# One of seven gate products replaced, for nine pairs of feature blocks, by seven products of quarters

## Chip, cores and metric

The kernel runs on one core of a Trainium2 chip. The metric is the device time of one execution in microseconds (us), the median of several runs. TensorE is called PE here, its weight loads PEld, VectorE DVE, ScalarE ACT, GpSimd POOL, and SP is the engine whose queue issues most DMAs.

## What is computed

One encoder block on 1024 tokens of width 1024, all in float32. Cut to its steps:

```python
h = rms_norm(x, norm1_g);  z = h @ w_in                     # 1024 x 2560
a, gate, q, k, v = split(z)
conv_out = silu(layer_norm(depthwise_conv31(a * sigmoid(gate)) + bias))
attn_out = neighbourhood_attention(rms_norm(q), rms_norm(k), v, rpb)
x = x + concat(conv_out, attn_out) @ w_out
h = rms_norm(x, norm2_g)
x = x + (silu(h @ w_gate) * (h @ w_up)) @ w_down             # D_FF = 2816
```

## The kernel before

Every matrix product is done in float32 precision out of rounded parts. An operand is split into a high part (an ACT cast to fp32r) and a low part (a subtraction, on DVE or POOL); `mac` (L110) then adds three matmuls to one PSUM tile, high x high (L112), high x low (L113) and low x high (L114). Each of them loads its own 128x128 weights.

The order on every engine is the order in which the Python program issues the instructions; nothing reorders it. Engines wait for each other through semaphores, and a tile from a pool waits until the last user of its slot is done. Pools that matter here: `G`, 25 slots of 128x1024; `ST`, 5 slots of 128x512; in PSUM `mm` (4 banks), `tp` (2 banks) and `cv` (one tile of two banks).

**First block (L522 to L543).** Eleven calls on `ones` (L250) run on PE while the first loads land; each is two matmuls in the trace. Then `four` adds, for the first two token tiles of the key projection, three matmuls per `mac` in the order k, token tile. Its operands come from `h_split` (L270, x times the norm's gain, which comes with the load of `par`) and from `take_parts` (L162, the split of the first weights `wk0`).

**Gate stage (L1204 to L1224).** Gate and up projections are one 2x2 block product by Winograd's form of Strassen's scheme: for each of 22 feature blocks `i` seven products `m1` to `m7` instead of eight, each of four `mac`s (12 matmuls of 512 columns) with the tokens as the moving operand. The blocks are ordered in 11 pairs. `product` (L1075) issues a product's matmuls, `evac` (L1086) combines its PSUM result: m1 is copied to `g` by ACT, and m6, m2, m5, m7, m3, m4 add to what is there. Banks: A for m1 and m2, B for m6, m5 and m3 (both `mm`), D for m7 and m4 (`tp`). From block 2 on the order is m1, m6, m2, m5, m7, m3, m4. After each product `prep` (L964) issues the splits for a product some four later: `t_sums` on DVE (four subtractions per block), casts on ACT, low parts on POOL. `keep` (L1118) stores the results and forms sums for the down projection.

**`s_weave` (L1033)** puts transposes of the normalised tokens' sums (`s_T`) between the matmuls of the first products; for S2 two single 512-column pieces and one double one in `cv`.

**Last tile (L1309).** The last token tile of the last product is done in two halves of 256 columns, each six matmuls into its half of the one bank `A3d`, then an add on DVE and a store.

Of the kernel before, what the change touches and what calls it, by code (L numbers as in the profile page):

```python
# [12 lines left out]
P = 128  # L13
# [17 lines left out]
def layout(v):  # L31
    f = {k: np.asarray(a)[0] for k, a in v.items()}
    w_in = f["w_in"]
    ag = w_in[:, :2 * DC].reshape(KB, P, 8, P).transpose(2, 1, 0, 3)
    qkv = w_in[:, 2 * DC:].reshape(4, 2, P, 3, 512).transpose(3, 0, 2, 1, 4)
    gu = np.stack([f["w_gate"], f["w_up"]]).reshape(2, KB, P, FB, P).transpose(3, 0, 2, 1, 4)
    wd = f["w_down"].reshape(FB, P, D)
    par = np.concatenate([
        f["norm1_g"].reshape(KB, P).T,
        f["dw_kernel"].reshape(CW, 4, P).transpose(2, 1, 0).reshape(P, 4 * CW),  # L40
        f["dw_bias"].reshape(4, P).T,
        f["conv_ln_g"].reshape(4, P).T,
        f["conv_ln_b"].reshape(4, P).T,
        np.concatenate([f["q_norm_g"]] * 2)[:, None],
        np.concatenate([f["k_norm_g"]] * 2)[:, None],
    ], axis=1)
    out = {
        "x": f["x"],
        "xt": f["x"].T.reshape(4, 2, P, 2, 512).transpose(3, 0, 2, 1, 4),
        "ag": ag.reshape(8, P, KB * P),  # L50
        "qkv": qkv.reshape(3, 4, P, 1024),
        "wo": f["w_out"],
        "gu": gu.reshape(FB, 2, P, KB * P),
        "wd": wd,
        "g2": f["norm2_g"][None],
        "rpb": f["rpb"],
        "par": par,
    }
    return {k: np.ascontiguousarray(a) for k, a in out.items()}
# [8 lines left out]
def build(ctx, tc, a):  # L68
# [47 lines left out]
    def lr(w):  # L116
        return w[:, :512], w[:, 512:]
# [19 lines left out]
    def issue():  # L137
        if pos[0] < len(chunks):
            src, name, _, _ = chunks[pos[0]]
            if pos[0] not in raws:  # L140
                raws[pos[0]] = R(name + "r")
            d = raws[pos[0]]
            if len(src.shape) == 3:
                d = d.rearrange("p (k m) -> p k m", k=src.shape[1])
            for q in (0, 1) if name == "wk0" else (None,):
                sl = slice(None) if q is None else slice(q * 512, q * 512 + 512)
                (nc.scalar if q == 0 else nc.sync).dma_start(d[:, sl], src[:, sl])
            pos[0] += 1

    def take(n=1, ahead=True):  # L150
# [70 lines left out]
    def load_xt(h, kp, sl):  # L221
        if (h, kp) not in xr:
            xr[h, kp] = G(f"xt{h}{kp}").rearrange("p (k s) -> p k s", s=512)
        for ks in (slice(0, 1), slice(1, 2)) if (h, kp, sl) == (0, 0, FIRST) else (slice(0, 2),):
            nc.sync.dma_start(xr[h, kp][:, ks, sl], a["xt"][h, kp][:, ks, sl])
# [5 lines left out]
    par = T("par", [P, 146], 1, "par")  # L231
    nc.scalar.dma_start(par, a["par"])
    for kp in range(4):
        load_xt(0, kp, FIRST)
# [11 lines left out]
    pool.memset(ones, 1.0)  # L246

    run_up = tp("up")
    for _ in range(11):
        pe.matmul(run_up[:, :P], ones, ones, start=True, stop=True)  # L250
# [3 lines left out]
    dve.tensor_scalar(qgs, qg, HD ** -0.5, None, op0=OP.mult)  # L254
# [13 lines left out]
    r1 = T("r1", [P, 8], 1, "r1")  # L268

    def h_split(h, k, sl):  # L270
        src = xr[h, k // 2][:, k % 2, sl]
        hi, lo = [w[:, k, sl] for w in hT[h]]
        act.activation(hi, src, AF.Copy, scale=g1[:, k:k + 1])
        dve.scalar_tensor_tensor(lo, src, g1[:, k:k + 1], hi.bitcast(F32), OP.mult, OP.subtract)

    def bn_sum(t, ss=None):
        st, mv = T("bn", [P, 2, 6], 2, f"sb{t}"), SM(f"sv{t}", 2)
# [246 lines left out]
    def four(kp, js, ts):  # L524
        for j, t in ((j, t) for j in js for t in ts):
            k = 2 * kp + j
            mac(zs[t], [q[:, k, t * P:(t + 1) * P] for q in hT[0]],
                [q[:, j * 512:(j + 1) * 512] for q in wn[1][kp]], k == 0, k == KB - 1)

    for kp in range(4):  # L530
        parts = []
        take_parts(parts, 2, dve)
        for j in range(2):
            h_split(0, 2 * kp + j, FIRST)
            parts[j]()
        for j in range(2):
            h_split(0, 2 * kp + j, SECOND)
        if kp == 1:
            for t in range(4):
                load_x(t)  # L540
        if kp < 3:
            four(kp, (0, 1), (0, 1))
            four(kp, (0, 1), (2, 3))  # L543
    take(1, False)
    ss = SM("s123", 2)
    stats1(0)
# [415 lines left out]
    tasks = list(products)  # L962

    def prep(n=1):  # L964
        for _ in range(n):
            if not tasks:
                return
            i, p = tasks.pop(0)
            if i < 2:
                if i == 1 and p in ("m6", "m5"):  # L970
                    t_sums(i, (1, 2) if p == "m6" else (3, 4))
            elif p == "m1":
                t_sums(i, (1, 2))
            elif p == "m6":
                t_sums(i, (3, 4))
            b = {"m1": (0, 0), "m2": (0, 1), "m3": (1, 1)}.get(p)
            n = {"m5": 0, "m6": 1, "m7": 2, "m4": 3}.get(p)
            src = lr(raw_gu[i, b[0]])[b[1]] if b else lr(tsum[i, n // 2])[n % 2]
# [12 lines left out]
            if i > 1 and p == "m3":  # L991
                load_gu(i + 2, 0)
# [19 lines left out]
    def s_T(n, kb):  # L1012
        if kb == 0:
# [18 lines left out]

    def s_weave(n):  # L1033
        skip = lambda: None
        parts = [lambda kb=kb: s_T(n, kb) for kb in range(3)]
        woven.extend([skip, skip, skip, skip, parts[0], parts[1], prep, parts[2]] if n == "S2" else
                     [parts[0], skip, parts[1], skip, parts[2]])

    g2b = G("g2b")
# [34 lines left out]

    def product(i, p):  # L1075
        w = {"m1": "A", "m2": "A", "m7": "D", "m4": "D"}.get(p, "B")
        if p in ("m1", "m6", "m7"):
            bank[i, w] = (tp if w == "D" and i > 1 else mm)(f"{w}{i}")
        acc, (th, tl), s = bank[i, w], top.pop((i, p)), sop[LEFT[p]]
        for k in range(HK):  # L1080
            mac(acc, [q[:, k * P:(k + 1) * P] for q in (th, tl)], [s[h][k] for h in range(2)],
                k == 0 and p in ("m1", "m6", "m7"), k == HK - 1)
            weave()
        return acc

    def evac(i, p, acc):  # L1086
# [7 lines left out]
            dve.tensor_tensor(u2[i], acc, l, OP.add)  # L1094
        elif p == "m2":
            sl[i] = ST(f"sl{i}") if i < 2 else acc
            act.activation(sl[i], acc, AF.Silu)  # L1097
        elif p == "m5":
            dve.tensor_tensor(r, acc, l, OP.add)  # L1099
# [105 lines left out]
    for n, (i, p) in enumerate(products):  # L1205
# [11 lines left out]
            late.pop(0)()  # L1217
        if extra and p in ("m2", "m5", "m7", "m6"):
            extra.pop(0)()
        prep({0: 0, 1: 0, 2: 0, 3: 2, 4: 0, 5: 3}.get(n, 1))  # L1220
        if i == FB - 1 and p in ("m2",):
            for q in range(4):
                load_item(q)
# [23 lines left out]
    def quarter(w, o, t):  # L1247
        return w[:, o + t * 512:o + t * 512 + 512]

    def finish(p, t, half=None):  # L1250
        acc = (GA if p in ("m1", "m2", "m7", "m4") else GB)[t]
        if p == "m1":
            if t == 0:
# [10 lines left out]
            dve.tensor_tensor(quarter(om["u"], 2048, t), acc, quarter(om["m1"], 2048, t), OP.add)  # L1264
        else:
            w = {"m7": quarter(om["u"], 2048, t), "m3": quarter(om["m1"], 2048, t), "m4": quarter(om["u"], 0, t)}[p]
            if half is None:
                dve.tensor_tensor(w, acc, w, OP.add)
                store(p, t, w)
            else:  # L1270
                sl = slice(half * 256, half * 256 + 256)
                dve.tensor_tensor(w[:, sl], acc[:, sl], w[:, sl], OP.add)
                store(p, t, w[:, sl], (nc.scalar, nc.sync)[half], half * 256)
# [5 lines left out]
    def down(n, t, cols=slice(0, 512)):  # L1279
        p, k = items[n]  # L1280
        acc, q = (GA if p in ("m1", "m2", "m7", "m4") else GB)[t], ops[n]
        mac(acc[:, cols], [q[:, h, t * P:(t + 1) * P] for h in range(2)], [q[:, 2 + h, cols] for h in range(2)],
            k == 0 and p in ("m1", "m6", "m7"), k == QF - 1)

    for s, p in enumerate(SEQ):
# [12 lines left out]
        for ts in ((0,), (1,), (2,)) if p == SEQ[-1] else ((0,), (1,), (2, 3)):  # L1298
# [6 lines left out]
                prep_items(1)  # L1305
            if p == "m7" and 0 in ts:
                add_res("m4", 3)

    for half in range(2):  # L1309
        for k in (QF - 2, QF - 1):  # L1310
            down((len(SEQ) - 1) * QF + k, 3, slice(half * 256, half * 256 + 256))
        finish(SEQ[-1], 3, half)


# [12 lines left out]
```

## Time and profile before

| | |
|---|---|
| runs | 1048.42, 1048.45, 1048.51 us, median 1048.45 us |
| the profiled execution | 1048.49 us, span 1046.6 us from the first to the last instruction |
| PE | 1040.2 us busy (99%), 5096 matmuls; weight loads 853.1 us (82%) |
| DVE, ACT, POOL | 694.3 us (66%), 452.6 us (43%), 382.2 us (37%) |
| DMA | 144.06 MB, mean 138 GB/s |
| granted TensorE clock | 0.999 |

A row of the timeline gives start and duration in us, engine, line, operation, output <- inputs, count, and in brackets the idle time of the engine just before, with what ended it. A row of groups gives count, busy us and mean ns of one, then the idle time just before. Matmuls overlap in the record, so the pace of PE is the distance between starts, not the duration.

### The profile page before, as it was taken

Reading aid. Unit: us, or ns where it says so; the run is one execution under the profiler, and the core shown is the slowest. Engines: PE = TensorE matmul, PEld = TensorE weight load, DVE = VectorE, ACT = ScalarE, POOL = GpSimd, SP = SyncE. Lnnn points to the kernel's source line nnn. Section 1 sums busy time; section 2 is a strip of 40 time slices with the busy share of each in tenths; the row PEclk is TensorE's granted clock in tenths of the full one; section 3 lists DMA queues with packets and bytes.
Section 4 is the critical chain, followed back from the end, with each engine's and each line's share of the span. In section 5 each row is a group of like instructions: output and inputs, shape, how many; then the busy total and the mean of one; then the engine's idle time right before and its main releaser. Section 6 shows DMA issues by size and latency. Waiting matters only on the chain.

```text
span 1046.6 us, 14146 instructions
## 1 busy us (share of the span) xinstructions
PE 1040.2 (99%) x5096; PEld 853.1 (82%) x5096; DVE 694.3 (66%) x1028; ACT 452.6 (43%) x988; POOL 382.2 (37%) x301
## 2 busy tenths in 40 slices
PE   9999999999999999999999999999999999999998
PEld 8888888877777887888888888888888888888886
DVE  5788997886754266774564655655546567858874
ACT  7465348837866134523323232233232444433431
POOL 1036765524640301455545545454555200002310
PEclk9999999999999999999999999999999999999999
DMA  9326781247216422132333232232232597633741
GB/s 350 156 69 208 225 258 42 76 158 260 74 52 150 141 81 81 61 111 94 108 116 108 79 131 101 71 132 99 97 125 80 189 324 271 212 101 102 237 130 45
DMA packets 69174, 144.06 MB, mean 138 GB/s; under 512 B 13169, under 2 KB 22129, under 8 KB 68465
## 3 DMA queue, kind: packets, MB, share of 16 engines
q1 hardware_dynamic: 67088, 139.82, 40.3%
q10 hardware_dynamic: 2016, 3.35, 1.0%
q8 instruction: 40, 0.66, 0.3%
q14 instruction: 30, 0.24, 0.1%
HBM read 103.99 MB, written 44.76 MB: 142 GB/s over the span
## 4 chain that ended last, share of the span: by engine, by line
PE 98%; DVE 1%; ACT 1%; issue 0%; POOL 0%; DVEq 0%; POOLq 0%
PE B L114 6%; PE B L112 6%; PE B L113 6%; PE z L112 4%; PE z L113 4%; PE z L114 4%; PE A L112 4%; PE D L114 4%; PE A L114 4%; PE D L112 4%; PE A L113 4%; PE D L113 4%; PE gl L114 3%; PE gl L112 3%; PE gl L113 3%; PE p L676 2%
## 5 line engine op out<-in xcount | busy, mean ns | idle before, releaser
L336 DVE SCALAR_TENSOR_TENSOR cv<-u,par,cv 128x1009 f32<-128x1009 f32 (+14 forms) x92 | 117.5, 1277 | 2.3
L362 POOL TENSOR_TENSOR pa<-pa,pr 128x1022 f32<-128x1022 f32 (+5 forms) x24 | 58.0, 2416 | 48.6 <-ACT pr L361 44.7
L104 ACT CAST op<-sr 128x512 fp32r<-128x512 f32 x77 | 47.7, 619 | 53.5 <-PE B2d L114 26.7
L108 DVE TENSOR_TENSOR op<-sr,op 128x512 fp32r<-128x512 f32 x77 | 59.0, 766 | 16.1 <-ACT op L104 16.0
L1099 DVE TENSOR_TENSOR g<-B,g 128x512 f32<-128x512 f32 x22 | 15.2, 691 | 78.5 <-PE B L114 78.5
L1277 POOL TENSOR_TENSOR ou<-ou,resm 128x512 f32<-128x512 f32 x8 | 12.5, 1576 | 141.8 <-DMA resm<-xd 141.8
L1108 ACT ACTIVATE D<-D 128x512 f32<-128x512 f32 x22 | 12.8, 582 | 113.6 <-DVE D L1107 113.6
L1094 DVE TENSOR_TENSOR u<-B,g 128x512 f32<-128x512 f32 x22 | 15.2, 691 | 62.2 <-PE B L114 62.2
L104 ACT CAST op<-wd 128x512 fp32r<-128x512 f32 x66 | 40.9, 619 | 30.0 <-DVE wd L1186 17.4
L955 DVE TENSOR_TENSOR ts<-gu,ts 128x512 f32<-128x512 f32 x44 | 51.0, 1158 | 0.8
L108 DVE TENSOR_TENSOR op<-wd,op 128x512 fp32r<-128x512 f32 x66 | 49.4, 749 | 1.6
L665 POOL TENSOR_SCALAR e<-e,rs 128x288 f32<-128x288 f32 (+1 forms) x64 | 34.0, 546 | 42.0 <-DVE rs L663 41.8
L654 ACT ACTIVATE e<-e,mx 128x288 f32<-128x288 f32 (+1 forms) x64 | 36.5, 571 | 18.8 <-DVE mx L649 18.8
L1097 ACT ACTIVATE A<-A 128x512 f32<-128x512 f32 x20 | 11.6, 582 | 75.7 <-PE A L114 75.7
L649 DVE CUSTOM_DVE_ANT_0 e<-s,tab 128x288 f32<-128x288 f32 (+1 forms) x64 | 28.7, 504 | 13.6 <-PE s L636 13.6
L955 DVE TENSOR_TENSOR ts<-gu 128x512 f32<-128x512 f32 x22 | 34.2, 1552 | 0.0
L389 ACT ACTIVATE sq<-z,r 128x64 f32<-128x64 f32 x96 | 28.4, 330 | 5.2 <-PE z L114 5.2
L361 ACT ACTIVATE pr<-u,par 128x1022 f32<-128x1022 f32 (+5 forms) x24 | 27.0, 1138 | 1.6 <-ACT vs L419 1.6
L1006 POOL TENSOR_TENSOR xn<-xn,xn 128x512 f32<-128x512 f32 x4 | 6.8, 1712 | 56.8 <-DVE sn L1006 51.2
L676 PEld LDWEIGHTS p<-ident,e 128*96 128x96 f32 (+1 forms) x192 | 20.6, 133 | 7.1 <-POOL e L665 6.3
L112 PE MATMUL B2d<-op 128*128 128x512 f32 x66 | 25.8, 391 | 0.0
L114 PE MATMUL B2d<-op 128*128 128x512 f32 x66 | 25.7, 389 | 0.0
(1041 smaller groups left out, 3469.9 us busy)
## 6 DMA issues: line engine op xcount, KB each, us to landing
gu<-in_gu SPq DMA_DIRECT2D x44, 512.0 KB
sr<-sd SPq DMA_DIRECT2D x77, 256.0 KB
sd<-sd SPq DMA_DIRECT2D x22, 512.0 KB
wd<-in_wd SPq DMA_DIRECT2D x44, 256.0 KB
sd<-g SPq DMA_DIRECT2D x33, 256.0 KB
x<-in_x SPq DMA_DIRECT2D x16, 512.0 KB
xd<-x SPq DMA_DIRECT2D x8, 512.0 KB
resm<-xd SPq DMA_DIRECT2D x16, 256.0 KB
```

Source lines behind the costliest of these rows:

```text
L104: act.copy(hi, src)
L108: eng.tensor_tensor(*[w[..., sl] for w in (lo, src, hi.bitcast(F32))], OP.subtract)
L112: pe.matmul(acc, lh, rh, start=start, stop=False, skip_group_check=True)
L113: pe.matmul(acc, lh, rl, start=False, stop=False, skip_group_check=True)
L114: pe.matmul(acc, ll, rh, start=False, stop=stop, skip_group_check=True)
L336: dve.scalar_tensor_tensor(acc[:, o], uc[:, i], dwk[:, c, t:t + 1], acc[:, o], OP.mult, OP.add)
L362: pool.tensor_tensor(pa[:, o], pa[:, o], pr[:, o], OP.add)
L649: dve.tensor_tensor_reduce(out=es[i][:, hh], in0=s[hh], in1=tab[rh, cb][2 * hp + hh], scale=-1.0, scalar=3.0e38, op0=OP.add, op1=OP.min, a ...
L654: act.activation(e, e, AF.Exp, bias=mx.pop((i, hh)), scale=-1.0, accum_out=sums[i][:, hh:hh + 1])
L665: pool.tensor_scalar(es[i][:, hh], es[i][:, hh], rs[:, hh:hh + 1], 1.0, op0=OP.mult, op1=OP.mult)
L676: pe.transpose(pt[:m, g * P:(g + 1) * P], es[i][:, hh, g * m:(g + 1) * m], ident)
L955: dve.tensor_tensor(o, l, r, OP.subtract)
```

## The change

For the nine pairs of blocks 4 and up, m1 is not computed as a product of its own. m1 of both blocks of a pair is one product of (256 features) x (512 inputs) x (512 tokens); it is now cut into quarters, and the same scheme of seven products is applied once more (`PARTS`, P1 to P7). Each part is two `mac`s of 256 columns, six matmuls. The seven parts are issued after seven successive products of the pair in front (`parts_at`), from the fourth of its twelve products on. For them:

- the weights that m1 needs are loaded once more for each pair (`load`, two DMAs of 256 KB on SP), added up by DVE (four 128x256 operations) and split by ACT and POOL (3.5 splits of 512 columns instead of the two of m1);
- the tokens' quarters are added up and split once (`tok_sums`), in POOL's queue, one job after each of products 10 to 22;
- results are combined by two ACT copies and five DVE additions of 128x256 per pair, into what was m1's place in `g`;
- the m1 products, their splits and their ACT copies go. m2 starts its own bank, and DVE adds `g` to it before SiLU; A of a pair now lies in `cv`, and two `mm` banks are used by the parts.

The transposes for S2 are four single pieces in `tp` banks. In the first block, the first 128x256 of x and two columns of gain come in one load of their own (`xa`), the first half of `wk0` is issued ahead of `par`, 9 calls on `ones` replace 11, and `first_two` issues high x high and low x high of both token tiles ahead of high x low. The scaling of `qgs` moves behind the first block. In the last tile, what is in bank A3 is added by DVE while other tiles are computed, and the two halves go to two other banks.

```diff
+        "xa": np.concatenate([xt[0, 0, :, 0, :256], f["norm1_g"][:2 * P].reshape(2, P).T], axis=1),
...
+    nc.sync.dma_start(xa, a["xa"])
+    nc.scalar.dma_start(raws[0][:, :512], chunks[0][0][:, :512])
     nc.scalar.dma_start(par, a["par"])
...
-    for _ in range(11):
+    for _ in range(9):
         pe.matmul(run_up[:, :P], ones, ones, start=True, stop=True)
...
+    def first_two(j):
+        for part in range(2):
+            for t in range(2):
+                hi, lo = [q[:, j, t * P:(t + 1) * P] for q in hT[0]]
+                wh, wl = [q[:, j * 512:(j + 1) * 512] for q in wn[1][0]]
+                if part == 0:
+                    pe.matmul(zs[t], hi, wh, start=j == 0, stop=False, skip_group_check=True)
+                    pe.matmul(zs[t], lo, wh, start=False, stop=False, skip_group_check=True)
+                else:
+                    pe.matmul(zs[t], hi, wl, start=False, stop=False, skip_group_check=True)
...
-    products += [(i, p) for i in range(2, FB) for p in ORDER]
+    products += [(i, p) for i in range(2, FB) for p in ORDER if i < 4 or p != "m1"]
+    PARTS = ("P1", "P6", "P2", "P5", "P7", "P3", "P4")
+    starts = {i: products.index((i, "m6")) for i in range(4, FB, 2)}
+    parts_at = {n0 - 9 + s: (i, p) for i, n0 in starts.items() for s, p in enumerate(PARTS)}
+    LEAD = {"load": 8, "P1": 1, "P6": 2, "P7": 2, "P4": 2}
...
+    def prep_part(i, p):
+        if p == "load":
+            raw4[i] = G(f"qr{i}")
+            for b in range(2):
+                nc.sync.dma_start(raw4[i][:, b * 512:(b + 1) * 512], a["gu"][ms[i + b], 0][:, :512])
+            return
...
+                dve.tensor_tensor(o, l, r, op)
+            split(*quad[i, 1], sum4[i][:, :512], (pool,))
...
+    def part(i, p):
+        for k in range(2):
+            mac(acc, [w[:, k * P:(k + 1) * P] for w in l], [w[:, k] for w in r],
+                k == 0 and p in ("P1", "P6", "P7"), k == 1)
...
+        if p in ("P1", "P2"):
+            act.copy(o, acc)
+        else:
+            dve.tensor_tensor(o, acc, {"P4": u, "P7": o}.get(p, c1), OP.add)
...
-        two = kb == 2
+        two = kb == 2 and n != "S2"
...
+        if first and w == "A" and i > 3:
+            if i % 2 == 0:
+                pair_a[0] = lr(cv(f"A{i}"))
+            bank[i, w] = pair_a[0][i % 2]
...
+            if i > 3:
+                dve.tensor_tensor(acc, acc, l, OP.add)
             act.activation(sl[i], acc, AF.Silu)
...
+        if n in parts_at:
+            part(*parts_at[n])
+        if n >= 10 and tok_jobs:
+            job = tok_jobs.pop(0)
...
+            if p == SEQ[-1] and 1 in ts:
+                finish(p, 3)
     for half in range(2):
+        acc, cols = GB[half][:, :256], slice(half * 256, half * 256 + 256)
...
+        dve.tensor_tensor(w, acc, w, OP.add)
+        store(SEQ[-1], 3, w, (nc.scalar, nc.sync)[half], half * 256)
```

More of the change, by code (lines that the diff above doesn't have):

```diff
@@ L540, in build @@
                 load_x(t)
+        if kp == 0:
+            first_two(0)
+            first_two(1)
         if kp < 3:
-            four(kp, (0, 1), (0, 1))
+            if kp > 0:
+                four(kp, (0, 1), (0, 1))
             four(kp, (0, 1), (2, 3))
+    dve.tensor_scalar(qgs, qg, HD ** -0.5, None, op0=OP.mult)
     take(1, False)
@@ new lines, in build, with quarter_of, tok_sums, full @@
+    tok4, tmp4, pair_a = {}, {}, [None]
+    def quarter_of(q):
+        k, c = divmod(q, 2)
+        return [w[:, 2 * k:2 * k + 2, c * 256:c * 256 + 256] for w in h2]
+    def tok_sums():
+        g = [G(f"qt{n}").rearrange("p (q k s) -> p q k s", q=2, s=256) for n in range(2)]
+        xa, xb, xc, xd4 = g[0][:, 0], g[0][:, 1], g[1][:, 0], g[1][:, 1]
+        def full(o, q):
+            hi, lo = quarter_of(q)
+            pool.tensor_tensor(o, hi.bitcast(F32), lo.bitcast(F32), OP.add)
+        def parts(n, src):
+            if n == 4:
+                tok4[n] = quarter_of(1)
+            else:
+                t = G(f"qT{n}", F32R).rearrange("p (w k s) -> p w k s", w=2, s=256)
+                tok4[n] = [t[:, 0], t[:, 1]]
+            split(*tok4[n], src, (pool,))
+        sub = lambda o, l, r: pool.tensor_tensor(o, l, r, OP.subtract)
+        return [lambda: full(xa, 1), lambda: full(xb, 0), lambda: full(xc, 3), lambda: sub(xb, xa, xb),
+                lambda: sub(xa, xc, xa), lambda: sub(xc, xc, xb), lambda: parts(2, xc), lambda: parts(1, xb),
+                lambda: parts(3, xa), lambda: full(xd4, 2), lambda: sub(xd4, xd4, xc), None, lambda: parts(4, xd4)]
@@ L969, in prep @@
+    def prep(n=1, upto=None):
+        while tasks and (n > 0 if upto is None else tasks[0][0] <= upto):
+            n -= 1
+            i, p = tasks.pop(0)[1]
+            if p[0] != "m":
+                prep_part(i, p)
+                continue
             if i < 2:
@@ L1034, in s_weave @@
         skip = lambda: None
[L1035 to L1036 removed]
+        parts = [lambda kb=kb: s_T(n, kb) for kb in range(4 if n == "S2" else 3)]
+        woven.extend([skip, skip, skip, skip, parts[0], parts[1], prep, lambda: (parts[2](), parts[3]())] if n == "S2" else
                      [parts[0], skip, parts[1], skip, parts[2]])
@@ L1081, in product @@
             mac(acc, [q[:, k * P:(k + 1) * P] for q in (th, tl)], [s[h][k] for h in range(2)],
-                k == 0 and p in ("m1", "m6", "m7"), k == HK - 1)
+                k == 0 and first, k == HK - 1)
             weave()
```

106 lines of the change are left out of this document (73 added, 33 removed).

## The prediction, made before the changed kernel ran

> **What bounds the kernel.** I read the busy shares of the page, then the chain that ended last, then the gate stage in stretches.
>
> ```profile
> PE 1040.2 (99%) x5096; PEld 853.1 (82%) x5096; DVE 694.3 (66%) x1028; ACT 452.6 (43%) x988; POOL 382.2 (37%) x301
> ...
> PEclk9999999999999999999999999999999999999999
> ...
> PE 98%; DVE 1%; ACT 1%; issue 0%; POOL 0%; DVEq 0%; POOLq 0%
> ```
>
> PE is busy all along at full clock, and 98% of the chain is PE. A busy PE need not be a PE at its pace, so the matmuls have to be counted. The stretches show it (busy us and count of PE, PEld, DVE, ACT, POOL; clock; DMA share; GB/s): a long one of the gate stage, one pair of blocks in it, and the stretch in which the token sums will fall.
>
> ```profile
> 480.00:800.00 320.00, 320.00 (x1413) 264.99 (x1412) 182.44 (x219) 92.09 (x168) 161.01 (x119) 1.00 0.30 102
> 561.90:600.00 38.10, 38.10 (x170) 31.55 (x169) 21.68 (x27) 11.00 (x20) 19.07 (x15) 1.00 0.31 104
> 444.00:484.00 40.00, 40.00 (x178) 33.10 (x177) 24.47 (x32) 12.98 (x25) 20.25 (x15) 1.00 0.30 106
> ```
>
> 320 us for 1413 matmuls of 512 columns is 0.2265 us each, without a gap over 117 products. So in this stage PE sets the time, and a matmul less is 0.2265 us less as long as operands and banks stay ahead. The other engines have room: DVE 57% of a pair, POOL 50%.
>
> **The pace of a 256-column matmul.** The whole sum hangs on it, and the last tile of this very kernel shows it.
>
> ```profile
> 1039.93 0.39 PE L113 MATMUL A2d<-op 128*128 128x512 f32 x1
> 1040.16 0.39 PE L114 MATMUL A2d<-op 128*128 128x512 f32 x1
> 1040.38 0.28 PE L112 MATMUL A3d<-op 128*128 128x256 f32 x1
> 1040.50 0.28 PE L113 MATMUL A3d<-op 128*128 128x256 f32 x1
> 1040.62 0.28 PE L114 MATMUL A3d<-op 128*128 128x256 f32 x1
> ...
> 1040.97 0.28 PE L114 MATMUL A3d<-op 128*128 128x256 f32 x1
> 1041.77 0.39 PE L112 MATMUL A3d<-op 128*128 128x256 f32 x1 [0.52 <-DVE ou L1272]
> ...
> 1042.47 0.28 PE L114 MATMUL A3d<-op 128*128 128x256 f32 x1
> ```
>
> From 1040.38 to 1040.97 are five steps, 0.118 each: half of 0.2265 would be 0.113, so a short matmul carries some 0.005 more. The step from 512 to 256 columns (1040.16 to 1040.38) is a normal one. The step back from 256 to 512 is not shown; I take 0.12 for it, with 0.113 and 0.2265 as its ends.
>
> **Gate stage, PE.** m1 of blocks 4 to 21 goes: 18 products of 12 matmuls, 216 x 0.2265 = 48.9 us. Added are 9 pairs x 7 parts x 6 = 378 matmuls of 256 columns; a part is 6 x 0.118 to 0.12, 0.713 us, so 63 x 0.713 = 44.9 us. The balance is -4.0 us. With the ends of the step back it is -4.4 to +2.7 (63 steps dearer by 0.107 at most); I stay at -4.0, since both neighbours of that step are normal and every matmul loads its own weights at either size.
>
> The Trainium skill, "TensorE: Matmul & The Clock Gate", section "Back-to-back issue gap", gives columns / 2.4 + 2.5 ns for a matmul alone, 215.8 and 109.2 ns, by which this term would be -5.3 us; the row has more for both.
>
> **What the gate stage adds elsewhere.** Rows for DVE in 480 to 800 us, for POOL in the pair, for the two 256-column additions of the last tile, and for the final store:
>
> ```profile
> L955 DVE TENSOR_TENSOR ts<-gu 128x512 f32<-128x512 f32 x17 | 28.0, 1650 | 0.0
> ...
> L1107 DVE TENSOR_TENSOR D<-D,u 128x512 f32<-128x512 f32 x17 | 11.8, 695 | 1.9 <-PE D L114 1.9
> L1099 DVE TENSOR_TENSOR g<-B,g 128x512 f32<-128x512 f32 x17 | 11.8, 692 | 67.5 <-PE B L114 67.5
> ```
> ```profile
> L1094 DVE TENSOR_TENSOR u<-B,g 128x512 f32<-128x512 f32 x17 | 11.8, 692 | 54.0 <-PE B L114 54.0
> ```
> ```profile
> L108 POOL TENSOR_TENSOR t8m<-ts,t8m 128x512 fp32r<-128x512 f32 x4 | 5.2, 1290 | 9.7 <-ACT t8m L104 9.7
> ```
> ```profile
> 1041.29 0.42 DVE L1272 TENSOR_TENSOR ou<-A3d,ou 128x256 f32<-128x256 f32 x1
> 1042.79 0.42 DVE L1272 TENSOR_TENSOR ou<-A3d,ou 128x256 f32<-128x256 f32 x1 [1.07 <-PE A3d L114]
> ```
> ```profile
> 1043.28 0.54 SPq L1244 DMA_DIRECT2D out_dram<-ou  x1
> ```
>
> DVE gets per pair five part additions (5 x 0.42), two additions ahead of SiLU (2 x 0.69) and four sums of 128x256, between 0.42 and 0.83 each (the PSUM row, and half of the slowest 512-column sum); I take 0.55. That is 5.7 us: 27.4 of 37.7 us, 73%. What hides it is the time that DVE waits for PE: 54.0 / 17 = 3.2 us ahead of each m6 (L1094) and 67.5 / 17 = 4.0 us ahead of each m5 (L1099). The tight places are banks: B of m6 has to be read while m2's 12 matmuls run, 2.7 us, before m5 may write it; m5's before m3, m7's before m4 likewise. Before the change the same held, and for A between m1 and m2 as well, which is gone. The worst spot is the first m6 of a pair: behind the m3 of the pair in front DVE has two additions (1.4), the four sums (2.2), and the m4 addition (0.7), 4.3 us, with 5.4 us of PE (m4, m6) to do it in; then 2.7 us are left for one addition of 0.69. That hides it with some 3 us to spare: cost 0. Banks q of the parts are read over more than 6 us, as two products and a part lie between two writes.
>
> The wait put in ahead of SiLU has ACT's casts for later products queued behind it, and POOL's subtractions behind these. They are issued four products ahead, 10.9 us, so a DVE addition of 0.69 costs nothing. POOL loses two subtractions per pair and gains 3.5: 19.1 + 2 = 21.1 of 37.7 us. SP gets two more loads of 256 KB per pair; gate weights and stores are queued behind them, at a DMA share of 0.30. They are issued eight products (22 us) ahead. Cost 0.
>
> The one place where I allow a stall is at the token sums. From 444 to 484 us POOL is busy 20.25 of 40; now come 12 operations of about 1.29 and 3.5 of the first pair's, 20 us more. POOL is then full for about 35 us, its lead of 10.9 us shrinks by a few us, and the low part of block 2's m7 arrives about when PE wants it. I put 0.3 us, ends 0 and 2.7 (twelve operations at 1.5 instead).
>
> **S2.**
>
> ```profile
> 415.52 1.01 ACT L104 CAST S<-sp 128x1024 fp32r<-128x1024 f32 x1 [1.16 <-PE sp L1025]
> ...
> 416.02 0.60 PE L1025 MATMUL sq<-ident,sn 128*128 128x128 f32 x4
> ...
> 417.15 0.39 PE L112 MATMUL B<-S,t0m 128*128 128x512 f32 x1
> 417.84 0.50 PE L113 MATMUL B<-S,t0m 128*128 128x512 f32 x1 [0.30 <-DVE S L108]
> ```
>
> PE loses 0.69 - 0.23 = 0.46 us at 417.15, since cast and subtraction are of the double piece; at 418.18 another 0.11. In single pieces they come in time. But S1's transposes of 416.02 then want the `tp` bank of S2's third piece, whose transposes end at about 415.1 and whose cast (0.6) and subtraction (0.7, both as in the first block's rows below) end at about 416.4: late next, a wait of 0.4. Balance -0.2, ends -0.5 and +0.4.
>
> **Last tile.** PE waits from 1040.97 + 0.12 to 1041.77, because the second half writes a bank that DVE still reads. With two banks it goes on at 0.12: -0.7 us. The first halves' first matmul also took 0.22 to the next; with it the last matmul starts at 1041.70 instead of 1042.47, -0.77. The addition and the store (1042.79, 1043.28) follow PE, so all of it counts.
>
> **First block.**
>
> ```profile
> 1.04 5.06 PE L250 MATMUL up<-ones 128*128 128x128 f32 x22 [1.04 <-POOL ones L246]
> 5.75 0.70 PE L112 MATMUL z<-wk0h,hT 128*128 128x512 f32 x1
> 6.35 0.50 PE L113 MATMUL z<-wk0l,hT 128*128 128x512 f32 x1
> 6.69 0.40 PE L114 MATMUL z<-wk0h,hT 128*128 128x512 f32 x1
> ...
> 9.02 0.39 PE L112 MATMUL z<-wk0h,hT 128*128 128x512 f32 x1
> ```
> ```profile
> 1.24 0.44 ACTq L147 DMA_DIRECT2D wk0r<-in_qkv  x1
> ...
> 4.95 0.62 ACT L104 CAST wk0h<-wk0r 128x512 fp32r<-128x512 f32 x1 [0.55 <-DMA wk0r<-in_qkv]
> ```
> ```profile
> 5.60 0.69 DVE L108 TENSOR_TENSOR wk0l<-wk0r,wk0h 128x512 fp32r<-128x512 f32 x1 [0.68 <-ACT wk0h L104]
> ```
>
> From the thirteenth matmul (9.02) back at 0.2265, the block behaves as if it had begun at 6.30 at full pace. `wk0`'s first half now is issued 0.45 us earlier (behind no `par`), so its cast ends at about 5.1; 18 instead of 22 matmuls on `ones` end by about 5.2; the subtraction (0.69) is needed four matmuls later instead of one. First matmul at about 5.3. The first steps of before are long (0.60, 0.34), the clock or the waits, and part of that stays. I take -0.5; ends -0.9 and +0.3 (`xa` or the clock later). `qgs` waits for `par` behind the block instead of in front: nothing.
>
> **Sum.** Against the profiled execution's 1048.49 us (span 1046.6 and 1.9 around it; median of the runs 1048.45): -4.0 - 0.8 - 0.5 - 0.2 + 0.3 = -5.2, so 1043.3 us.
>
> **Rivals.** (1) Slower: DVE falls behind at the pair's first m6, because m1's 2.7 us between m4 and m6 are gone and four sums have come. For it speaks DVE's 73% and that its sums swing from 0.69 to 1.65 us; against it the 3 us worked out above. The bank then holds up m5 once per pair; from 0.81 us per pair ((5.2 + 2.1) / 9) the change loses. At 1.2 us: 1054. Chance 0.06. (2) Slower: weight loads set the pace of short matmuls.
>
> ```profile
> L114 PEld LDWEIGHTS A3d<-op 128*128 128x128 f32 x46 | 8.6, 188 | 1.7
> ```
>
> At 0.188 per part matmul, 378 cost 71.1 us: +22.2 instead of -4.0, 1069.5. From 0.1295 (48.9 / 378) the parts gain nothing. The six steps of 0.118 speak against it, though only twelve such matmuls exist before. The same section of the skill also says that in a stream with weight loads the pace is set by both, about 81 ns at 128 columns and 131 at 512; in between, some 98 at 256, the balance would be +8.7. This trace has 226.5 and 118. Chance 0.03. (3) The joints cost: each part's step back to 512 columns takes 0.06 more, or POOL is late at the token sums by its full 2.7: 1046 to 1047. Chance 0.10. (4) The parts are hidden or cancelled otherwise, and only the ends of the kernel gain, about 1047.3. Chance 0.03. My forecast, 1042.2 to 1045, has 0.78.
>
> **Numbers.** The range is 1042.2 to 1046.4: below, the better ends of first block (-0.4), S2 (-0.3) and token sums (-0.3); above, the milder half of (3). About 0.2% (2.1 us) is what a measurement of this kernel can tell from no change. Faster by more: 0.78, half of (3), so 0.84; within: the rest of (3) and (4), 0.07; slower: (1), (2), 0.09.
>
> **What would show it.** PE with 5254 matmuls; parts of six starts 0.118 to 0.12 apart and the next product one such step later; a pair in about 37.7 us; no idle time on PE with DVE as releaser at m5; DVE near 73% in a pair; first key matmul near 5.3; no gap in the last twelve. I am wrong if a part takes over 0.78 us, if PE waits for `tp` or q banks in every pair, or if POOL's lead runs out for more than a product.

## The result, and the profile after

The changed kernel takes 1046.49 us (median of 17 runs, 1046.08 to 1047.21), the kernel before 1048.47 us in the same series; the ratio is 0.9981, interval 0.9975 to 0.9988. It is faster by 2.0 us where 5.2 were forecast, and lies just above the range. The profiled execution took 1046.49 us, with a span of 1044.6.

The page's busy times, then the chain that ended last, by engine:

```profile
PE 1036.8 (99%) x5254; PEld 857.2 (82%) x5254; DVE 732.3 (70%) x1129; ACT 457.3 (44%) x1011; POOL 429.6 (41%) x331
...
PE 95%; DVE 3%; ACT 1%; issue 1%; POOL 0%; DVEq 0%; ACTq 0%; POOLq 0%
```

PE has the 5254 matmuls that the change implies. But the chain now has 3% DVE and 1% of bare issue where it had 1% and 0%. PE's busy time fell by 3.4 us and the span by 2.0, so PE idles longer. The view of waits on PE says where:

```profile
PE A L114 <- DVE g L1224: 1.1, 1, 1.1
PE up L255 <- POOL ones L251: 1.0, 1, 1.0
PE B L114 <- DVE u L1213: 0.8, 1, 0.8
```

The second line is the start of the kernel and stood there before. The other two are new, each a single wait on DVE. To place them, take two matmuls that both kernels have: the first of block 2's m1 and the first of the down projection. Here they are in the timeline, the two of before and then the two of after:

```profile
451.18 0.39 PE L112 MATMUL A<-h,t2m 128*128 128x512 f32 x1
831.98 0.39 PE L112 MATMUL A0d<-op 128*128 128x512 f32 x1
```
```profile
449.63 0.39 PE L114 MATMUL A<-h,t2m 128*128 128x512 f32 x1
830.48 0.39 PE L114 MATMUL A0d<-op 128*128 128x512 f32 x1
```

Between them lies all that the new m1 touches on PE: 380.80 us before, 380.85 after. The large edit has gained nothing. The changed kernel is ahead by 1.55 us before this stretch and by 1.50 behind it; what is won is won at the kernel's ends.

Inside the stretch, 216 long matmuls went. Both waits lie where the first quartered pair is prepared, among the products of blocks 2 and 3, and where the token sums stand. Three rows of PE's timeline (rows between them left out):

```profile
455.07 0.39 PE L114 MATMUL A<-h,t2m 128*128 128x512 f32 x1
458.73 0.50 PE L114 MATMUL B<-S,t2m 128*128 128x512 f32 x1 [0.78 <-DVE u L1213]
472.41 0.47 PE L114 MATMUL A<-h,t3m 128*128 128x512 f32 x1 [1.06 <-DVE g L1224]
```

A product of twelve takes 2.72 us; the one at 455.07 takes 3.66 to the next start. The second wait, ahead of block 3's m1, is a step of 1.34 from 471.07 to 472.41. With the one slow step behind each, they cost 1.05 + 1.30 = 2.35 us. DVE in front of the first of them:

```profile
452.85 0.91 DVE L1015 TENSOR_TENSOR qs<-qr 128x256 f32<-128x256 f32 x1
453.80 1.40 DVE L1015 TENSOR_TENSOR qs<-qs,qr 128x256 f32<-128x256 f32 x1
455.12 1.52 DVE L1015 TENSOR_TENSOR qs<-qr 128x256 f32<-128x256 f32 x1
456.56 1.51 DVE L1015 TENSOR_TENSOR qs<-qr,qs 128x256 f32<-128x256 f32 x1
457.99 0.68 DVE L1213 TENSOR_TENSOR u<-B,g 128x512 f32<-128x512 f32 x1
```

The four weight sums of the first pair take 5.3 us together. In the eight later pairs of 480 to 800 us the same sums run while POOL is idle and take 0.42 each. B is read at 457.99, and m5 has waited for that. In front of the second wait DVE reads block 2's B behind two sums of 512 columns:

```profile
469.89 1.78 DVE L979 TENSOR_TENSOR ts<-gu,ts 128x512 f32<-128x512 f32 x1
471.59 0.68 DVE L1224 TENSOR_TENSOR g<-B,g 128x512 f32<-128x512 f32 x1
```

The window from 448 to 474 us (busy us and count of PE, PEld, DVE, ACT, POOL; clock; DMA share; GB/s) has POOL without a gap and DVE almost so; one pair further on follows:

```profile
448.00:474.00 26.00, 24.16 (x111) 19.67 (x111) 25.38 (x25) 9.06 (x18) 26.00 (x17) 1.00 0.34 113
561.90:600.00 38.10, 38.10 (x190) 32.32 (x189) 25.49 (x38) 11.32 (x22) 22.32 (x16) 1.00 0.36 118
```

The other half of the loss is spread evenly. Around one part in steady state (PE's timeline):

```profile
702.18 0.28 PE L114 MATMUL q<-h,qa 128*128 128x256 f32 x1
...
702.78 0.28 PE L116 MATMUL q<-h,qa 128*128 128x256 f32 x1
702.90 0.40 PE L114 MATMUL B<-S,t15m 128*128 128x512 f32 x1
703.13 0.40 PE L115 MATMUL B<-S,t15m 128*128 128x512 f32 x1
703.37 0.39 PE L116 MATMUL B<-S,t15m 128*128 128x512 f32 x1
703.59 0.40 PE L114 MATMUL B<-S,t15m 128*128 128x512 f32 x1
703.83 0.39 PE L115 MATMUL B<-S,t15m 128*128 128x512 f32 x1
704.06 0.39 PE L116 MATMUL B<-S,t15m 128*128 128x512 f32 x1
```

The part takes 0.713 us, as forecast. Of the five steps behind it four are clearly too long: the median steps behind the parts are 233, 236, 228, 233, 231 ns and then 227. That is 0.027 us per part, without a wait, 63 x 0.0267 = 1.7 us. A pair of blocks takes 37.82 us where it took 38.08 before.

So this stretch changes by -48.96 (216 x 0.2267) + 44.9 (63 parts) + 1.7 (steps behind them) + 2.35 (waits) = 0.0 us.

### The profile page after: what moved, and what is told of

The parts are those of the page before. It is cut to its first block, busy times and chain, and to the rows that moved or that the text cites. A ratio compares the mean times of both kernels' runs of the same rounds, so it can differ in the third digit from the quotient of the medians.

```text
span 1044.6 us, 14712 instructions
## 1 busy us (share of the span) xinstructions
PE 1036.8 (99%) x5254; PEld 857.2 (82%) x5254; DVE 732.3 (70%) x1129; ACT 457.3 (44%) x1011; POOL 429.6 (41%) x331
## 4 chain that ended last, share of the span: by engine, by line
PE 95%; DVE 3%; ACT 1%; issue 1%; POOL 0%; DVEq 0%; ACTq 0%; POOLq 0%
PE B L114 5%; PE B L115 5%; PE B L116 5%; PE z L114 4%; PE z L116 4%; PE z L115 4%; PE D L114 4%; PE D L115 4%; PE D L116 4%; PE gl L116 3%; PE gl L115 3%; PE gl L114 3%; PE p L700 2%; PE o L719 2%; PE A L114 2%; PE A L115 2%
## 5 line engine op out<-in xcount | busy, mean ns | idle before, releaser
L110 DVE TENSOR_TENSOR op<-sr,op 128x512 fp32r<-128x512 f32 x77 | 55.5, 721 | 18.7 <-ACT op L106 18.7
L979 DVE TENSOR_TENSOR ts<-gu,ts 128x512 f32<-128x512 f32 x44 | 47.6, 1082 | 0.8
L1217 DVE TENSOR_TENSOR A<-A,g 128x512 f32<-128x512 f32 x18 | 12.6, 700 | 22.2 <-PE A L116 22.2
L979 DVE TENSOR_TENSOR ts<-gu 128x512 f32<-128x512 f32 x22 | 27.7, 1261 | 0.0
L114 PE MATMUL B2d<-op 128*128 128x512 f32 x66 | 25.8, 391 | 0.0
```

Source lines behind the costliest of these rows:

```text
L110: eng.tensor_tensor(*[w[..., sl] for w in (lo, src, hi.bitcast(F32))], OP.subtract)
L114: pe.matmul(acc, lh, rh, start=start, stop=False, skip_group_check=True)
L979: dve.tensor_tensor(o, l, r, OP.subtract)
```

## The experiments

Beside each time stands the ratio to the kernel before, as it ran in the same series (1048.47 to 1048.62 us), and the length of the stretch from block 2's m1 to the down projection. That length is the sharper figure, since the first key matmul alone falls between 4.9 and 5.4 us in kernels with the same start. A diff below shows the lines that matter; `...` stands for what is left out.

| kernel | median us | ratio and interval | stretch us |
|---|---|---|---|
| before | 1048.47 | 1 | 380.80 |
| changed | 1046.49 | 0.9981 (0.9975 to 0.9988) | 380.85 |
| ends alone | 1046.78 | 0.9983 (0.9974 to 0.9991) | 380.80 |
| gate alone | 1048.34 | 0.9998 (0.9989 to 1.0006) | 380.84 |
| token sums left out | 1044.29 | 0.9960 (0.9947 to 0.9974) | 378.76 |
| sums of the first pair left out | 1046.02 | 0.9975 (0.9965 to 0.9986) | 380.13 |
| from block 6 | 1045.89 | 0.9976 (0.9966 to 0.9986) | 379.94 |
| from block 6, parts in twos | 1046.27 | 0.9977 (0.9968 to 0.9987) | 380.02 |
| block 3's A elsewhere | 1046.80 | 0.9985 (0.9975 to 0.9994) | 380.84 |
| weight sums two by two | 1049.34 | 1.0007 (0.9999 to 1.0016) | 383.30 |
| token sums in halves | 1047.86 | 0.9994 (0.9985 to 1.0003) | 381.83 |
| from block 6, block 5's A elsewhere | 1044.69 | 0.9963 (0.9951 to 0.9976) | 378.72 |
| the same, parts in twos | 1044.29 | 0.9960 (0.9946 to 0.9975) | 378.24 |
| from block 4, both edits | 1045.83 | 0.9976 (0.9966 to 0.9985) | 380.11 |

**The change in two halves.** The ends alone:

```diff
-    starts = {i: products.index((i, "m6")) for i in range(4, FB, 2)}
+    starts = {}       # m1 in full products for all blocks, no token sums
...
```

> The kernel before with the edits of the first block, of S2's single pieces and of the last tile, and m1 in full products as before. Theory (the edits at the ends bring some 2.0 us and the gate's change nothing on balance): 1046.4 to 1046.8, level with the changed kernel. By the forecast's terms (0.5 + 0.2 + 0.8): 1047.0. By a rival, that the ends bring less where the gate is not changed (the S2 gain belongs to the new order of tasks): 1047.2 or more.

And the gate alone, with the first block, S2 and the last tile of before:

> The kernel before with the quarters of m1 and the token sums alone; first block, S2 and last tile as before. Theory (matmuls bring 2.4, two stalls at the token sums take 2.3): 1048.2 to 1048.6, level with the kernel before, with PE held up twice by DVE between 455 and 475 us, by 0.9 and 1.1 us. By the forecast's terms (-4.0 + 0.3): 1044.8.

Measured: 1046.78 and 1048.34 us. The first is 1.8 us under the kernel before, as the theory had it. The second cannot be told from the kernel before, and in it both waits of PE are there again:

```profile
PE A L113 <- DVE g L1212: 1.1, 1, 1.1
PE up L251 <- POOL ones L247: 1.0, 1, 1.0
PE B L113 <- DVE u L1201: 0.8, 1, 0.8
```

The gain of the changed kernel is that of its ends.

**Without the token sums.**

```diff
         if n == 10:
-            tok_jobs = tok_sums()
+            tok4.update({1: quarter_of(0), 2: quarter_of(1), 3: quarter_of(3), 4: quarter_of(1)})
+            tok_jobs = []
```

> The changed kernel with the sums of tokens left out: the parts read other quarters of the tokens as they are, so this part of the computation is missing; every matmul, weight sum and addition is as in the changed kernel. Theory (GpSimd, full with the token sums, makes VectorE's operations of two SBUF inputs two to three times as long, so VectorE is late twice): VectorE's four weight sums of the first pair take 0.42 to 0.6 us instead of 0.9 to 1.5, both stalls go, 1044.1 to 1044.5. Rival (VectorE's added work alone, the four weight sums and the additions, overloads it at the first pair): the stalls stay, 1046 to 1046.5. The forecast's term for the token sums (0.3) gives 1046.2.

Measured: 1044.29 us, the stretch 2.1 us shorter than in the changed kernel. No wait of PE on DVE over 0.3 us is left in it, and the same four weight sums read:

```profile
452.57 0.41 DVE L1015 TENSOR_TENSOR qs<-qr 128x256 f32<-128x256 f32 x1
453.01 0.42 DVE L1015 TENSOR_TENSOR qs<-qs,qr 128x256 f32<-128x256 f32 x1
453.35 0.42 DVE L1015 TENSOR_TENSOR qs<-qr 128x256 f32<-128x256 f32 x1
453.69 1.52 DVE L1015 TENSOR_TENSOR qs<-qr,qs 128x256 f32<-128x256 f32 x1
```

DVE does the same work at the same place; what is gone is POOL's token sums, with the four casts on ACT that belong to them. DVE's added work by itself overloads nothing: the rival falls.

**Without the first pair's weight sums.**

```diff
-                                (s3, w11, w21, OP.subtract), (s4, w12, s2, OP.subtract)):
+                                (s3, w11, w21, OP.subtract), (s4, w12, s2, OP.subtract)) if i > 4 else ():
...
```

> The changed kernel without VectorE's four weight sums of the first pair: that pair's quarters are used unsummed, so this part of the computation is missing. Theory (GpSimd being full is what makes VectorE late): the stall of 0.9 us at about 458 us goes, as the four sums of 5.3 us stood there; the one of 1.1 us at about 472 us stays in the main: 1045.4 to 1045.8. Rival (the four sums are the whole cause, and the delay is carried from the first place to the second): both go, 1044.2 to 1044.5. Rival (GpSimd itself is late, the sums only stand beside it): nothing moves, 1046.5.

Measured: 1046.02 us. The first wait is gone, and the second is a step of 1.60 where it was 1.34. So the two do not have one cause; the theory's time was 0.2 us too low, as the second wait grew.

**Quarters from block 6 on, token sums behind every second product.**

```diff
-    starts = {i: products.index((i, "m6")) for i in range(4, FB, 2)}
+    starts = {i: products.index((i, "m6")) for i in range(6, FB, 2)}
...
-        if n >= 10 and tok_jobs:
+        if n >= 14 and n % 2 == 0 and tok_jobs:
```

> The changed kernel with m1 of blocks 4 and 5 in full products again, the quarters from block 6 on (8 pairs instead of 9), and the twelve token sums issued one behind every second product instead of behind each. Theory (the token sums stood too close together): no PE step above 0.3 us between 455 and 475 us, 2.3 us won and one pair's 0.26 us lost: 1044.3 to 1044.7. Rival (the token sums slow VectorE wherever they stand): shorter stalls remain, 1045 to 1046.

Measured: 1045.89 us, a miss of the theory by more than 1 us and within the rival's range. The first wait is gone, but the second has moved along to the last full block, 5: a step of 1.25 us at 508.54, again behind two sums of 1.78 and 1.77 us beside a busy POOL. That one thus belongs to the passage from full products to quarters and not to the crowd of token sums alone.

**Parts two at a time.**

```diff
-    parts_at = {n0 - 9 + s: (i, p) for i, n0 in starts.items() for s, p in enumerate(PARTS)}
+    parts_at = {n0 - 9 + s // 2 * 2: [(i, p) for p in PARTS[s:s + 2]] for i, n0 in starts.items() for s in (0, 2, 4, 6)}
...
```

> As the run with the quarters from block 6 on, with the parts put in two at a time (P1 and P6, P2 and P5, P7 and P3, P4 alone): four returns to 512 columns per pair instead of seven, as many short matmuls. Theory (each return to 512 columns costs 0.027 us, whatever the number of short matmuls ahead of it): 8 x 3 x 0.0267 = 0.64 us faster than with single parts, and 0.027 behind twelve short matmuls as behind six. Rival (each short matmul costs some 0.0045 us, paid back behind the part): the delay behind twelve is 0.053, and the time is the same within 0.1 us. Rival (parts close together wait for banks or for GpSimd's operands): slower, with steps above 0.3 us inside the parts.

Measured: 1046.27 us. The steps behind twelve short matmuls are 233, 236, 228, 233, 231 ns, the same as behind six, so the 0.027 us is paid per return to 512 columns and not per short matmul. But a pair takes 37.76 instead of 37.82 us: 0.06 saved and not 0.08, because the second part's first step is 0.120 and not 0.113. That would be 0.5 us over eight pairs; the step at block 5's m1 grew from 1.25 to 1.88 and took it back.

**Another bank for the last full block's A.** In the changed kernel, A of block 3 comes from the four banks that B and the parts' q share, and PE had waited for a read of B.

```diff
-        if first and w == "A" and i > 3:
-            if i % 2 == 0:
+        if first and w == "A" and i > 2:
+            if i % 2 == 0 or i == 3:
```

> The changed kernel with bank A of block 3 taken from the two-bank tile of the later blocks instead of from the four banks which B and the parts' q share. Theory (m1 of block 3 waits for B of block 2, since two q banks now lie between them in the rotation, and DVE reads B late behind two sums of 1.8): the stall of 1.1 us at about 472 us goes, no new one comes, 1045.3 to 1045.6. Rival (VectorE is late for everything, the bank is only where it shows first): PE waits at the next operand or bank of block 3, 1046.0 to 1046.5.

Measured: 1046.80 us, the stretch 380.84: the theory is wrong here. The rival has it right that the next operand is late, but that operand is POOL's and not VectorE's, and the time lies above its range too. PE starts m1 in time and halts two matmuls later, and POOL shows why:

```profile
471.17 0.40 PE L115 MATMUL A<-h,t3m 128*128 128x512 f32 x1
472.59 0.50 PE L116 MATMUL A<-h,t3m 128*128 128x512 f32 x1 [1.03 <-POOL t3m L110]
```
```profile
469.12 1.74 POOL L110 TENSOR_TENSOR qc<-qs,qc 128x512 fp32r<-128x512 f32 x1
470.81 1.72 POOL L110 TENSOR_TENSOR t3m<-gu,t3m 128x512 fp32r<-128x512 f32 x1
```

The bank and the low part of m1's weights were late at the same time. POOL's subtractions, 1.29 us in the row that the forecast went by, take 1.7 each.

**The weight sums two by two**, s3 and s4 only when P7 needs them:

```diff
-            for o, l, r, op in ((s1, w21, w22, OP.add), (s2, s1, w11, OP.subtract),
-                                (s3, w11, w21, OP.subtract), (s4, w12, s2, OP.subtract)):
+            for o, l, r, op in ((s1, w21, w22, OP.add), (s2, s1, w11, OP.subtract)):
```

> The changed kernel with the four weight sums issued two by two: the pair that P6 needs where all four stood, the pair that P7 needs three parts later. Theory (four sums of 1.4 us in a row are what makes VectorE's read of B late at about 458 us): that stall of 0.9 us goes, and as VectorE and GpSimd stay full to 474 us, the 2.9 us of the other two sums come due ahead of m1 of block 3, so that stall stays or grows to 2: 1045.6 to 1046.6. Rival (any spread relieves both): 1044.5 to 1045.2.

Measured: 1049.34 us, 2.7 above the theory's end. The first wait went, but PE then stood 2.5 us ahead of m4 of block 2, with s3, s4 and two more sums in DVE's queue ahead of the read of bank D. And the loss went on after it (DVE's read of D, PE's timeline, then the windows, where the column behind POOL is the granted clock):

```profile
470.20 0.68 DVE L1224 TENSOR_TENSOR g<-D,g 128x512 f32<-128x512 f32 x1
471.02 0.47 PE L114 MATMUL D<-A,t2m 128*128 128x512 f32 x1 [2.51 <-ACT t3m L106]
...
472.03 0.63 PE L115 MATMUL D<-A,t2m 128*128 128x512 f32 x1
```
```profile
471.00:472.00 1.00, 0.97 (x4) 0.85 (x5) 1.00 (x2) 1.00 (x4) 1.00 (x2) 1.00 0.00 0
472.00:473.00 1.00, 1.00 (x4) 0.78 (x3) 1.00 (x1) 0.60 (x2) 1.00 (x1) 0.51 0.23 90
```

The bracket names a cast for block 3 that ended at 470.99, which m4 of block 2 does not read; the read of D, which it needs, ended at 470.88. From 472.03 to 475.4 the clock is at half and eight matmuls take 0.427 us each: 1.6 us more, on top of the idle 2.5.

**The token sums in halves**, each POOL operation cut into two of 256 columns:

```diff
-            pool.tensor_tensor(o, hi.bitcast(F32), lo.bitcast(F32), OP.add)
+            for k in range(2):
+                pool.tensor_tensor(*[w[:, k] for w in (o, hi.bitcast(F32), lo.bitcast(F32))], OP.add)
```

> The changed kernel with each of GpSimd's token sums and token subtractions in two operations of 256 columns instead of one of 512. Theory (VectorE's operation of two SBUF inputs waits out the GpSimd operation that runs, whole): of the four weight sums at 453 to 458 us those that stand against a halved operation take 0.9 instead of 1.45, the stall at 458 us shrinks by 0.5 or more, 1045.4 to 1046.2. Rival (both engines share the bandwidth at a rate): the sums stay at 1.4 to 1.5, and GpSimd's fixed part per operation makes it later: 1046.5 to 1048.

Measured: 1047.86 us. The theory's durations came, its time did not:

```profile
452.81 0.85 DVE L1015 TENSOR_TENSOR qs<-qs,qr 128x256 f32<-128x256 f32 x1
453.58 0.96 DVE L1015 TENSOR_TENSOR qs<-qr 128x256 f32<-128x256 f32 x1
454.46 1.51 DVE L1015 TENSOR_TENSOR qs<-qr,qs 128x256 f32<-128x256 f32 x1
```
```profile
452.46 1.80 POOL L1040 TENSOR_TENSOR qt<-h,h 128x256 f32<-128x256 f32 x2
454.22 1.47 POOL L110 TENSOR_TENSOR t2m<-ts,t2m 128x512 fp32r<-128x512 f32 x1
```
```profile
PE B L116 <- POOL t2m L110: 1.0, 1, 1.0
PE D L116 <- POOL t2m L110: 0.8, 1, 0.8
PE A L116 <- POOL t3m L110: 0.7, 1, 0.7
```

Beside halved POOL operations (0.9 each) a weight sum takes 0.85 to 0.96, beside a whole one that had just begun still 1.51. DVE's two waits went. But two halves take POOL mostly 1.8 to 2.3 us where one whole took 1.7, so POOL falls behind, and PE waits for its operands at three places. In that the rival is right, and the time lies in its range.

**From block 6 on, with the bank.** Both of the causes at once: sums at half the rate, and A of block 5 from the two-bank tile (`i > 4` and `i == 5` in the lines shown for block 3). With single parts:

> As the run with the quarters from block 6 on and single parts, with bank A of block 5 taken from the two-bank tile. Theory (token sums at half their rate leave GpSimd's operands in time, so here the bank alone held PE up, where in the changed kernel GpSimd's operand was late behind it): the 1.0 us at m1 of block 5 goes, 1044.7 to 1045.0, and the run with two parts at a time and the same bank is faster by what 24 saved returns are worth, 0.47 by its trace. Rival (the next operand is late, as with block 3): 1045.5 to 1046.

and with two parts at a time:

> As the run with the parts two at a time from block 6 on, with bank A of block 5 taken from the two-bank tile. Theory: the step of 1.88 us at m1 of block 5 goes, and the 24 returns saved show: 1046.3 - 1.65 = 1044.5 to 1044.8; against the run with single parts from block 6 on, whose own stall there is 1.0, 1.3 to 1.7 less. Rival: the wait goes on to the next operand of block 5, 1045.5 to 1046.3.

Measured: 1044.69 and 1044.29 us, the first at the lower end of its theory and the second 0.2 below it. PE has no wait left in the gate stage; all waits of 0.2 us or more in the second of them are

```profile
PE up L255 <- POOL ones L251: 1.0, 1, 1.0
PE s L660 <- DVE e L707: 0.3, 1, 0.3
PE sq L1139 <- DVE S L110: 0.3, 1, 0.3
PE z L115 <- DVE wk1l L110: 0.2, 1, 0.2
```

The saved returns show as 0.48 us of the stretch, for 0.47 expected. The last is the best version: 4.2 us under the kernel before and 2.2 under the changed one, though one pair fewer is quartered.

**From block 4 on, with both edits.**

> The changed kernel (quarters from block 4 on, token sums behind every product) with bank A of block 3 from the two-bank tile and the parts two at a time, the first two behind m4 of the last full block. Theory (GpSimd full from 448 to 474 us sets it): a stall of some 0.9 at 458 us stays, one of up to 1.2 on an operand from GpSimd stays, 27 returns saved bring 0.5: 1045.3 to 1046.2, slower than from block 6 on with the same two edits (1044.3). Rival (bank and parts together suffice): 1043.9 to 1044.4.

Measured: 1045.83 us, inside the theory's bounds. DVE holds PE up 0.8 us as before, POOL 0.4. With the token sums behind every product neither edit suffices.

## Why the prediction was wrong, step by step

**The token sums (+0.3) were the largest miss: 2.35 us.** The prediction saw that POOL would be full and charged only POOL's own lead. It took the four weight sums at 0.55 us, between 0.42 and 0.83, half of a sum of 512 columns alone and beside POOL; they took 0.91 to 1.52. The step that failed for the first wait, 1.05 of the 2.35, is the halving. A DVE operation with two operands in SBUF does not slow in proportion to its columns; it waits out the POOL operation that is under way. The rows of before allowed this reading: the sums at L955 averaged 1650 ns, while the additions that read PSUM took 692 to 695 in the same stretch. In the changed kernel from 480 to 800 us, 33 sums of 512 columns (L979) ran with POOL idle, median 0.691 us, and 33 with POOL at work all along, median 1.769. Of these 33, 17 took 1.77 to 1.80, eight 1.22 and eight 0.68 to 0.75: the last began as one POOL operation ended and were ahead of the next (a sum at 566.00 took 0.683, and the POOL operation of 566.01 took 1.82). The 16 additions `u<-B,g` all ran beside POOL and took 0.692. "Some 3 us to spare" therefore held at every pair but the first, where POOL was full.

The Trainium skill, "SBUF — State Buffer", section "Who interferes with whom", states this: a VectorE instruction with two SBUF inputs contends with a GpSimd instruction that reads SBUF, and whichever comes second is blocked until the first is done, while one with at most one SBUF input does not contend. The trace agrees with both halves of it (1.769 against 0.691, and 0.692), and the run with halved token sums shows that the length of the GpSimd operation sets the wait. By that rule a sum beside a full POOL could have been costed at up to 0.42 + 1.29 = 1.7 us from rows of before, four of them at 6.8 in place of 2.2. DVE's 4.3 us would then have been 8.9, and 9.6 with the addition behind them, against 8.1 of PE (m4, m6 and m2): a stall of up to 1.5 us instead of none.

The second wait, 1.30, has another failed step: the banks at "cost 0". The prediction looked at the banks of the quartered pairs. Block 3's A, the last one that a full m1 writes, still waits for a read of B, and DVE does that read behind two whole sums that the full POOL has stretched to 1.79 and 1.78. From block 6 on the same wait of 1.0 us went when A alone was moved, and without the token sums the step there was 0.33 instead of 1.34. That POOL's operands come late was foreseen in rival (3), "by its full 2.7". It did happen: the run with another bank for block 3 shows it, 1.03 us, behind the DVE wait. What no rival had is that both happen at the same place, so that removing either moves nothing.

**The step back to 512 columns (0.12 taken) was right, and the term was still short by 1.7 us.** The step itself is 0.120. The bounds of 0.113 and 0.2265 were put on that one step alone; the price lies in four of the five steps behind it. The predicted pair of "about 37.7" took 37.82, and the term is -2.4 instead of -4.0.

**Banks and DVE in the steady pairs: right.** DVE was to have 27.4 of 37.7 us and has 25.5 of 38.1, POOL 21.1 and has 22.3; PE waits for neither. Rival (1), DVE behind at the first m6 of every pair with its bank holding up m5, came once, as the first wait, and in no steady pair. Rival (2) did not come: parts of 0.713 us leave no room for weight loads at 0.188.

**S2 (-0.2): -0.72.** The wait for the `tp` bank came as worked out, 0.44 for 0.4. The gain was too small: PE's steps before of 0.52, 0.40 and 0.33 us at 419.30, 420.15 and 420.55 were not in the working, and go as well.

**First block (-0.5): -0.85 in this profile.** The first key matmul starts at 4.90 and not at 5.3; the thirteenth and all that follow keep the lead. The size is in part luck: in the twelve profiles with this start (the changed kernel's among them) the first of block 0's m6 on S2, at 415.24 before, lies between 414.13 and 415.64, so that the lead there is -0.4 to 1.1 us, median 0.7.

**Last tile (-0.8): -0.78 up to the last matmul**, at 1040.19 for 1042.47, without a gap. But the span ends 4.43 us behind that start where it ended 4.18 behind before. These 0.25 us were not foreseen, and they are not chance: 4.4 to 4.5 in all twelve profiles with the new last tile, 4.1 to 4.2 in the two with the old one. The second half's store now follows the first closely; whether that is the cause no run took apart.

In sum: 0.85 + 0.72 + 0.78 - 0.25 = 2.1 us from the ends and nothing from the gate, as the two runs of the halves show (1.8 and 0.25, the latter within its interval of nothing). That is the outcome of rival (4), which had a chance of 0.03, with the ends at 2.1 where it had 1.2. Of the signs that the prediction named, one came, PE idle at m5 with DVE as releaser; none of the three by which it would have called itself wrong did. Two of its sums are slightly off and change nothing here: twelve operations at 1.5 instead of 1.29 are 2.5 us and not 2.7, and 0.78 with half of 0.10 is 0.83 and not 0.84.

## What to carry to other kernels

A price taken for an operation holds only beside the neighbour that it had: before VectorE gets more two-operand work in SBUF, look at what GpSimd does in that stretch, and cost each such operation at the length of a GpSimd operation if GpSimd is full. A change that pays a little in each of many rounds can lose it all at the one passage into the new pattern, so cost that passage by itself: its sums, the rotation of its banks, and the engine that prepares its operands. When two things are late at once, removing one shows nothing; the runs that counted took away both.

## What the runs showed of the hardware that was not expected

Each return from 256 to 512 columns costs 0.027 us, in four of the five steps behind it (233, 236, 233 and 231 ns where 227 is normal), after six short matmuls as after twelve. It is not proper to the parts: behind the wait at 458.73 the first step is 337 ns, and then 235, 229, 232, 231 and 227 follow. Why is open.

In the run with the weight sums two by two, an idle stretch of PE of 2.5 us was enough for the granted clock to fall to 0.5, one us after work had begun again and for 3.4 us. Waits of 1.0 to 1.5 us did not do that in any run here. The Trainium skill, "TensorE: Matmul & The Clock Gate", section "Part 1: The HAM clock gate (the "warmup" mystery)", has half clock after an idle window of about 3.4 us, counted in free-running windows; here 2.5 us were enough.

The length of the idle stretch by itself does not decide it. At the end of the kernel before, the clock fell 1.1 us after the last matmul. The stretches of full clock in the traces last 467.63, 573.44, 1034.24, 1037.65 or 1041.07 us, which are 137, 168, 303, 304 and 305 times 3.413, so in these records the clock changes only at steps of 3.413 us. Counted along these steps, the clock fell behind every one in which PE had been busy for at most 1.77 us (0.99 in the run two by two, 1.77 at the end of the kernel before) and behind none with 1.92 us or more (1.92 beside the longest of the other waits, 1.49 us). This is worked out from the records of the 14 kernels here, in which the ends of matmuls are modelled; nothing between 1.77 and 1.92 was met.

DVE and POOL, both at work on SBUF, took turns every 1.70 us (512 columns each, 1.74 to 1.79 from start to end) where 0.69 and 1.29 alone would add up to 1.98.
